# A bidirectional state-space mixer on one core: transposes on TensorE, stores off SP's queue, a moved sum, gates kept in DRAM, products on GpSimd

## The chip, the cores and the metric

The kernel runs on one core of a Trainium2 chip. The metric is the device time of one execution in microseconds (us). The kernel before was timed twice: 1167.71 and 1169.27 us, median 1168.49 us. Its trace comes from one further, profiled execution. The engines are named as in the profile: PE is TensorE, DVE is VectorE, ACT is ScalarE, POOL is GpSimd, SP is SyncE, which here only issues DMA (SPq is its queue of issues).

## What is computed

One pre-norm layer of a bidirectional state-space mixer over 1024 tokens of width 1024 (inner width 2048, 32 heads of 64 in 8 groups, state 128, chunks of 128 tokens), then a final norm:

```python
u = rmsnorm(x, norm_w)
proj = u @ w_in                       # 1024 x 6208
z, xbc, dt_raw = proj[..., :2048], proj[..., 2048:6144], proj[..., 6144:]
xbc = silu(depthwise_conv_centred(xbc, conv_w, conv_b))   # 5 taps
xs, bm, cm = x heads, B, C            # slices of xbc
dt = softplus(dt_raw + dt_bias); a = -exp(a_log)
y = xs * d_skip
for direction in range(2):            # 1: on flipped tokens
    y = y + ssd_scan(xs * dt, dt * a, bm, cm)     # chunked scan
y = y * silu(z)                       # the gate
y = y * rsqrt(mean(y*y per group) + EPS) * ssd_norm_w
out = rmsnorm(x + y @ w_out, final_norm_w)
```

## The kernel before

All products of float32 matrices are made of three matmuls on pairs of a rounded "hi" part and a "lo" rest: hi·hi, hi·lo, lo·hi. ACT casts the hi part (L129) and DVE or POOL subtracts it for the lo part (L130).

**Start** (0 to 75 us of the trace). x is normed and transposed into four blocks b11, b12, b21, b22 (channel half by token half); sums of blocks t1 to t4 are made, and the z gate of group 0 and dt are projected. b12 and this gate go to DRAM (`b12_d`, `gate_d`).

**Product phase** (75 to 514 us). The 4096 columns of x, B and C come in 16 pairs of 128-column tiles: for each group g first "BC" (one tile of B, one of C), then "x" (two tiles). `load_pair` loads a pair's weights on SP (L261) into `raw`, which has two buffers, one pair ahead, and makes seven combinations a11, s1, s2, a12, s3, s4, a22 (POOL's sums L273, ACT's casts, DVE's and POOL's lo parts). `pair_products` is a 2x2 block scheme with seven products of twelve 128x512 matmuls each (L295). They accumulate in two PSUM tiles c1 and c2 of 1024 columns, halves c11, c12, c21, c22. Product P5 (from s1 and t1) lies in a PSUM tile of its own and is copied to SBUF as `p5` (L324). Between products DVE adds `p5` to c12 (L330), ACT copies c12 to c22 (L331), and later DVE writes c21 = c22 − p5 (L335): the next product accumulates onto what these wrote. Then `conv` filters c1 and c2: one pass of ACT (L344), four of DVE (L350), tanh on ACT (L353), the closing product on DVE (L354). `keep_tm` turns x and B into token-major order: a DVE transpose in blocks of 32x32 (L362) and four DMAs on SP (L365) to `xb_d`, in pieces of 32 columns. B and C also go to `bc_d`, on SP (L463).

**Gap** (514 to 546.6 us). After the last pair b12 comes back from DRAM (L475), the gates of group 0 too (L640), and the z weights of group 1 (L484) are loaded and split.

**Scan phase** (546.6 to 1029 us). `z_stream` makes the z columns of groups 1 to 7: eight steps a group, each 24 matmuls 128x256 (L145). `gate_of` puts the gates into SBUF tiles of four chunks. `ssd_units(g)` yields 16 times: eight backward steps and eight forward chunks. A `state` multiplies xb by wdt to xw on DVE (L530) and PE multiplies it (L533); `update` carries the running state (L523, L525). `mix` makes the decay matrix of a chunk on ACT (L557, L562) and DVE (L559, L567). A forward chunk then makes pyo and pyd on PE (L600, L606), adds on DVE (L609, L619), multiplies by the gate on DVE (L624), takes the norm (square on ACT L626, power on POOL L85, scale on ACT L628), transposes on DVE (L631) and stores to `y_d` with four DMAs on SP (L634). z steps stand between the yields, at positions given by the tuple AT. Of the sixteen units of the output product (48 matmuls 128x512 each, L709: eight token tiles by two halves of the inner width), four of half 0 stand in the last group.

**Tail** (1029 to 1161 us). The other twelve units.

The framework orders each engine's instructions by a priority, which `high_priority` moves ahead.

## Time and profile before

| | us |
|---|---|
| median of two runs | 1168.49 |
| the profiled execution, its own time | 1162.74 |
| its span in the trace | 1161.0 |
| PE busy | 950.8 (82%) |
| DVE busy | 835.4 (72%) |
| ACT busy | 585.2 (50%) |
| POOL busy | 253.0 (22%) |

The profiled execution took 1.74 us more than its span, and 5.75 us less than the median. Busy times of PE are upper bounds of useful work: successive matmuls overlap in the trace, so the start of one to the start of the next says more than a duration.

### The profile page before, as it was taken

How to read it: one execution, taken by the hardware profiler on the slowest of the kernel's cores; microseconds unless marked ns; L12 is line 12 of the kernel's file. 1: busy time of each engine (PE TensorE's matmuls, PEld its weight loads, DVE VectorE, ACT ScalarE, POOL GpSimd, SP SyncE). 2: the span in 40 equal slices, each digit the busy share in tenths (PEclk: the TensorE clock that was granted, in tenths of full speed). 3: DMA queues.
4: the chain of work that ended last, by engine and by line, in shares of the span. 5: the costliest groups of instructions: out<-in, count | busy, mean ns of one | idle time of the engine just before them, and what ended most of it. 6: DMA issues, size and time to landing. Idle time of an engine off the chain costs nothing.

```text
span 1161.0 us, 15429 instructions
## 1 busy us (share of the span) xinstructions
PE 950.8 (82%) x4890; PEld 798.0 (69%) x4890; DVE 835.4 (72%) x1687; ACT 585.2 (50%) x1573; POOL 253.0 (22%) x228
## 2 busy tenths in 40 slices
PE   4894689588958966861999998989887779999997
PEld 4783467466736755651999987879775557888886
DVE  5547879848866884873789888888888886855423
ACT  4442344244334422421687877787877673744211
POOL 4359531245145304500000100010111000010000
PEclk9797899889979998995999999999995688999999
DMA  7221134433372345138766665676667657868531
GB/s 220 86 92 36 46 97 103 91 91 72 73 169 55 68 91 127 18 73 249 197 187 166 158 166 144 152 169 163 174 156 166 147 155 211 186 183 295 177 109 55
DMA packets 272915, 155.90 MB, mean 134 GB/s; under 512 B 176752, under 2 KB 244032, under 8 KB 272320
## 3 DMA queue, kind: packets, MB, share of 16 engines
q1 hardware_dynamic: 272832, 154.90, 51.0%
q8 instruction: 39, 0.64, 0.2%
q14 instruction: 44, 0.36, 0.1%
HBM read 113.70 MB, written 41.16 MB: 133 GB/s over the span
## 4 chain that ended last, share of the span: by engine, by line
PE 48%; DVE 18%; ACT 11%; DMA 8%; issue 7%; POOL 6%; SPq 1%; DVEq 0%; POOLq 0%; ACTq 0%
PE po L709 14%; PE x L295 9%; PE pz L145 9%; PE BC L295 6%; DMA fb<-rows_d 5%; PE pyd L606 3%; DVE x L350 3%; PE pyo L600 2%; ACT yo L617 2%; DVE B L350 2%; ACT fb L557 2%; PE sb L533 2%; DMA wz<-in_ssd_w_in_dram 2%; DVE C L350 2%; ACT fb L562 1%
## 5 line engine op out<-in xcount | busy, mean ns | idle before, releaser
L617 ACT ACTIVATE yo<-pyo,ecs 128x64 f32<-128x64 f32 x448 | 103.8, 310 | 19.5 <-PE pyo L600 16.9
L557 ACT ACTIVATE fb<-fb,cfb 128x128 f32<-128x128 f32 x256 | 83.2, 396 | 27.9 <-DMA fb<-rows_d 27.7
L562 ACT ACTIVATE fb<-fb,cfb 128x128 f32<-128x128 f32 x256 | 85.1, 394 | 21.6 <-DVE fb L559 21.3
L350 DVE SCALAR_TENSOR_TENSOR x<-x,prm,x 128x1022 f32<-128x1022 f32 (+1 forms) x64 | 81.7, 1276 | 14.9 <-ACT x L344 13.7
L606 PEld LDWEIGHTS pyd<-xb,mt 128*128 128x128 f32 x512 | 73.4, 214 | 19.8 <-ACT pyd L626 14.6
L609 DVE SCALAR_TENSOR_TENSOR y<-xb,coef,pyd 128x64 f32<-128x64 f32 x256 | 61.6, 272 | 32.5 <-PE pyd L606 32.3
L606 PE MATMUL pyd<-xb,mt 128*128 128x64 f32 x512 | 74.8, 295 | 11.5 <-ACT pyd L626 8.9
L559 DVE COPY_PREDICATED fb<-trif,fb 128x512 f32<-128x512 uint32 x64 | 47.1, 736 | 11.3 <-ACT fb L557 11.1
L145 PE MATMUL pz<-wz_0h,b11h 128*128 128x256 f32 (+1 forms) x60 | 20.1, 334 | 35.3 <-ACT wz_0h L129 32.4
L600 PE MATMUL pyo<-pf,ct 128*128 128x256 f32 x112 | 38.4, 426 | 12.7 <-DVE pf L525 9.8
L619 DVE TENSOR_TENSOR y<-y,yo 128x256 f32<-128x256 f32 x112 | 46.6, 417 | 3.1 <-ACT yo L617 2.9
L709 PE MATMUL po<-wo0h,yh 128*128 128x512 f32 x128 | 45.9, 434 | 2.5 <-ACT yh L129 2.5
L709 PE MATMUL po<-wo0l,yh 128*128 128x512 f32 x128 | 44.4, 427 | 2.6 <-DVE wo0l L664 2.6
L533 PE MATMUL sf<-xwf,xb 128*128 128x256 f32 x112 | 39.4, 437 | 8.2 <-ACT yo L617 6.0
L709 PE MATMUL po<-wo0h,yl 128*128 128x512 f32 x128 | 44.4, 422 | 1.9 <-DVE yl L130 1.9
L85 POOL TENSOR_TENSOR y_0r<-y_0m,neghalf 128x1 f32<-128x1 f32 x8 | 4.8, 603 | 188.3 <-DVE y_0m L82 188.3
L567 DVE TENSOR_TENSOR mt<-fb,pcb 128x512 f32<-128x512 f32 x64 | 43.4, 678 | 3.3 <-ACT fb L562 2.9
L350 DVE SCALAR_TENSOR_TENSOR B<-BC,prm,B 128x1022 f32<-128x1022 f32 (+1 forms) x32 | 40.9, 1279 | 2.8 <-ACT B L344 2.2
L533 PE MATMUL sb<-xwb,xb 128*128 128x256 f32 x112 | 38.0, 429 | 5.6 <-issue 2.2
L709 PE MATMUL po<-wo1h,yh 128*128 128x512 f32 (+1 forms) x136 | 42.2, 377 | 0.0
L709 PE MATMUL po<-wo1l,yh 128*128 128x512 f32 (+1 forms) x136 | 42.1, 377 | 0.0
L709 PE MATMUL po<-wo1h,yl 128*128 128x512 f32 (+1 forms) x136 | 42.1, 377 | 0.0
(1402 smaller groups left out, 3165.8 us busy)
## 6 DMA issues: line engine op xcount, KB each, us to landing
fb<-rows_d SPq DMA_DIRECT2D x128, 256.0 KB, 4.4
xb<-xb_d SPq DMA_DIRECT2D x64, 192.0 KB, 4.1
wz<-in_ssd_w_in_dram SPq DMA_DIRECT2D x16, 512.0 KB, 5.3
y_d<-yt SPq DMA_DIRECT2D x256, 32.0 KB, 2.3
wo<-in_ssd_w_out_dram SPq DMA_DIRECT2D x16, 512.0 KB, 4.9
...
```

Of the source, the lines that this page charges most:

```text
L145: nc.tensor.matmul(pz[:, 0:m], a, b, start=at == 0, stop=at == 3 * NK - 1)
L295: nc.tensor.matmul(ps, a[:, k, :], b[:, k, :], start=fresh and n == 0, stop=n == 11, skip_group_check=True)
L350: nc.vector.scalar_tensor_tensor(out=acc[:, o], in0=ps[:, i], scalar=w(k), in1=acc[:, o], op0=ALU.mult, op1=ALU.add)
L533: nc.tensor.matmul(ps[:, 0:CW], xb[:, CW:CW + P], xw, start=True, stop=True)
L557: nc.scalar.activation(out=ef[:, h], in_=ef[:, h], func=AF.Identity, bias=cfb[:, 1, c, hsl(g, h)])
L559: nc.vector.copy_predicated(ef, trif.bitcast(U32).unsqueeze(1).broadcast_to([P, HG, P]), fb[:, 0])
L562: nc.scalar.activation(out=ef[:, h], in_=ef[:, h], func=AF.Exp, bias=cfb[:, 0, c, hsl(g, h)])
L600: nc.tensor.matmul(pyo[:, d * CW:(d + 1) * CW], ct[:, tok], st, start=True, stop=True)
L606: nc.tensor.matmul(pyd[:, cs], mt[:, h, :], xb[:, cs], start=True, stop=True)
L609: nc.vector.scalar_tensor_tensor(out=y[:, cs], in0=xb[:, cs], scalar=coef[:, h:h + 1], in1=pyd[:, cs], op0=ALU.mult, op1=ALU.add)
L617: nc.scalar.activation(out=yo[:, cs], in_=pyo[:, d * CW + h * HD:d * CW + (h + 1) * HD], func=AF.Copy, scale=ecs[:, d, c, hsl(g, h)])
L709: nc.tensor.matmul(pos[i], l_, r_[:, cols[i]], start=k == 0 and a == 0, stop=k == NO - 1 and a == 2)
```

## The change

- **Turning.** `keep_tm` transposes x and B by eight matmuls against the identity on PE into two PSUM tiles, which ACT copies to SBUF (L371); one DMA on ACT's queue stores the tile in pieces of 128 columns. The stores of B and C to `bc_d` are issued by ACT too. This part is deferred: the transposes of a pair's two tiles stand in the next pair, after its fourth and its seventh product (`late`).
- **P5.** ACT copies c12 to c22 and c22 to c21 with nothing between; DVE adds `p5` to c12 and to c22 once, after the pair's products, ahead of the convolution (L341, L342).
- **Order of the combinations and tiles.** s2 and s4 are summed earlier; the sums share the ring of the weight tiles (10 for hi, 12 for lo).
- **End of the product phase.** The reload of b12 and the first z weights stand ahead of the last pair's convolution.
- **Gates.** All gates go to `gate_d` by DMAs issued by POOL (L526) and come back on SP, one chunk at a time (64 loads, L626).
- **Scan.** xw (112 operations) and y times gate (64) are on POOL. The transpose and store of a chunk's y stand behind the next chunk's scaling. xb has 8 buffers, not 9.
- **Fillers.** The z stream, the loads of the first half's w_out and the units of half 0 are one generator `fills`, which yields every 12 matmuls within a unit; AT has ten places a group, not eight. FIRST = 5 units of half 0 stand in the scan, not 4.

```diff
@@ load_pair
         put("a11", a11, False)
         s1 = combine("s1", a21, a22, ALU.add)
+        s2 = combine("s2", s1, a11, ALU.subtract)
         put("s1", s1, False)
-        s2 = combine("s2", s1, a11, ALU.subtract)
         put("s2", s2, False)
...
@@ pair_products
         product(c11, w["a12"], b21, False)
+        late(0)
         c2 = ptile(name + "2", w)
         c21, c22 = c2[:, 0:512], c2[:, 512:1024]
         with tc.high_priority(offset=HP):
-            nc.vector.tensor_tensor(out=c12, in0=c12, in1=p5, op=ALU.add)
             nc.scalar.copy(c22, c12)
         product(c22, w["s3"], t3, False)
         product(c12, w["s4"], b22, False)
         with tc.high_priority(offset=HP):
-            nc.vector.tensor_tensor(out=c21, in0=c22, in1=p5, op=ALU.subtract)
+            nc.scalar.copy(c21, c22)
         product(c21, w["a22"], t4, False)
-        return c1, c2
+        late(1)
+
+        nc.vector.tensor_tensor(out=c12, in0=c12, in1=p5, op=ALU.add)
+        return c1, c2, lambda: nc.vector.tensor_tensor(out=c22, in0=c22, in1=p5, op=ALU.add)
@@ keep_tm
-        tt = big(name, (P, 32, 32))
-        nc.vector.transpose(tt.rearrange("p b j -> p (b j)"), acc)
-        dst = xb_d[g].rearrange("(b i) c -> i b c", i=32)
-        for a in range(4):
-            nc.sync.dma_start(out=dst[:, :, off + 32 * a:off + 32 * a + 32],
-                              in_=tt[32 * a:32 * a + 32])
+        tm = big(name, (P, NC, P))
+        for q in range(2):
+            pt = pst(f"{name}p{q}")
+            for k in range(4):
+                nc.tensor.transpose(out=pt[:, k * P:(k + 1) * P],
+                                    in_=acc[:, (4 * q + k) * P:(4 * q + k + 1) * P], identity=ident)
+            nc.scalar.copy(tm[:, 4 * q:4 * q + 4], pt.rearrange("p (k n) -> p k n", k=4))
+        nc.scalar.dma_start(out=xb_d[g].rearrange("(k p) c -> p k c", p=P)[:, :, off:off + P], in_=tm)
@@ the loop over pairs
+                nc.scalar.dma_start(out=bc_d[g, i], in_=acc)
...
+        if nxt is None:
+
+            b12 = ublock(up, "v", "b12b")
+            for i, part in enumerate(b12):
+                nc.sync.dma_start(out=part.rearrange("p k t -> p (k t)").bitcast(F32), in_=b12_d[i])
+            wz1 = load_z(1)
...
+            if i:
+                join()
+            acc = conv(p_, 2 * g + i if nm == "x" else 16 + 8 * i + g, f"{nm}{i}_{g}")
+            left.append(keep(acc, g, nm, i))
@@ z_stream
+                        nc.gpsimd.dma_start(out=gate_d[g, :, c0:c0 + 4], in_=gt)
@@ state
-        nc.vector.tensor_tensor(out=h4(xw), in0=h4(xb[:, 0:CW]),
+        nc.gpsimd.tensor_tensor(out=h4(xw), in0=h4(xb[:, 0:CW]),
@@ ssd_units, a forward chunk
+            nc.sync.dma_start(out=gt, in_=gate_d[g, :, c])
...
-            nc.vector.tensor_tensor(out=y, in0=y, in1=gates[g, c // 4][:, c % 4], op=ALU.mult)
+            nc.gpsimd.tensor_tensor(out=y, in0=y, in1=gt, op=ALU.mult)
...
+            if c > 0:
+                store(c - 1, done)
+            done = y
@@ the order of the scan
-    AT = (2, 5, 8, 10, 11, 13, 14, 15)
-    every(stream, 2)
+    AT = (2, 6, 8, 9, 10, 11, 12, 13, 14, 15)
+    every(stream, 3)
```

How the change moves instructions. On SP in the middle of the product phase, the kernel before has the two halves of the load of wx2r (weights of pair x2) on both sides of group 1's last store and group 2's first ones:

```order
44 L365 DMA xb_d<-x1t_1469 32x32x32 x4
45 L261 DMA wx2r<-in_ssd_w_in_dram 128x8x128
46 L463 DMA bc_d<-B_1607 128x1024
47 L365 DMA xb_d<-Bt_1617 32x32x32 x4
48 L463 DMA bc_d<-C_1623 128x1024
49 L261 DMA wBC3r<-in_ssd_w_in_dram 128x8x128 x2
```

The same place of the changed kernel:

```order
28 L262 DMA wx2r<-in_ssd_w_in_dram 128x8x128 x2
29 L262 DMA wBC3r<-in_ssd_w_in_dram 128x8x128 x2
30 L262 DMA wx3r<-in_ssd_w_in_dram 128x8x128 x2
31 L262 DMA wBC4r<-in_ssd_w_in_dram 128x8x128 x2
32 L262 DMA wx4r<-in_ssd_w_in_dram 128x8x128 x2
```

No store stands between the weight loads of the pairs any more.

On SP at the end of the product phase, before:

```order
84 L365 DMA xb_d<-x0t_3336 32x32x32 x4
85 L365 DMA xb_d<-x1t_3351 32x32x32 x4
86 L475 DMA b12bh<-b_d 128x2048
87 L475 DMA b12bl<-b_d 128x2048
88 L640 DMA gate0r_3375<-gate_d 128x1024
89 L640 DMA gate0r_3377<-gate_d 128x1024
90 L484 DMA wz_0_3379<-in_ssd_w_in_dram 128x4x256
91 L484 DMA wz_1_3389<-in_ssd_w_in_dram 128x4x256
92 L540 DMA bt_3449<-bc_d 128x1024
```

and in the changed kernel:

```order
38 L262 DMA wx7r<-in_ssd_w_in_dram 128x8x128 x2
39 L442 DMA wz_0_3525<-in_ssd_w_in_dram 128x4x256
40 L442 DMA wz_1_3535<-in_ssd_w_in_dram 128x4x256
41 L442 DMA wz_0_3873<-in_ssd_w_in_dram 128x4x256
42 L442 DMA wz_1_3883<-in_ssd_w_in_dram 128x4x256
43 L494 DMA b12bh<-b_d 128x2048
44 L494 DMA b12bl<-b_d 128x2048
45 L442 DMA wz_0_4575<-in_ssd_w_in_dram 128x4x256
```

The z weights (wz) of group 1 stand right behind the last weight load, ahead of b12, and wait for no store.

On POOL in the first group's forward chunks the changed kernel has (the kernel before has only the rows of L85 there):

```order
176 L659 TENSOR_TENSOR y_0_3844<-y_0_3844,gt_0_3819 128x256
177 L85 TENSOR_TENSOR y_0r<-y_0m,neghalf 128x1
178 L553 TENSOR_TENSOR xwf_3_4151<-xb_3_3737,wdt 128x256
179 L659 TENSOR_TENSOR y_1_3943<-y_1_3943,gt_1_3917 128x256
180 L553 TENSOR_TENSOR xwf_4_4245<-xb_4_3701,wdt 128x256
181 L85 TENSOR_TENSOR y_1r<-y_1m,neghalf 128x1
182 L659 TENSOR_TENSOR y_2_4035<-y_2_4035,gt_2_4009 128x256
183 L553 TENSOR_TENSOR xwf_5_4337<-xb_5_3692,wdt 128x256
184 L526 DMA gate_d<-gate_4_3773 128x1024
```

xwf runs two chunks ahead of the gate's product there, and the store of a gate stands in the same queue.

## Rows read from the trace of the kernel before

**Rows 1.** Windows by stage: length; busy time (instructions) of PE, PEld, DVE, ACT, POOL; PEclk, DMA, GB/s.
```profile
159.00:514.00 355.00, 284.19 (x1152) 220.41 (x1152) 264.69 (x242) 133.89 (x186) 119.94 (x85) 0.93 0.38 86
514.00:546.00 32.00, 0.14 (x1) 0.00 (x0) 13.85 (x11) 3.41 (x4) 0.00 (x0) 0.57 0.57 160
546.00:1029.00 483.00, 432.20 (x2655) 382.70 (x2655) 401.68 (x1238) 354.44 (x1226) 42.08 (x62) 0.91 0.67 171
1029.00:1161.00 132.00, 125.43 (x572) 103.77 (x571) 53.43 (x75) 32.49 (x55) 7.13 (x10) 0.98 0.50 162
```

**Rows 2.** Timeline of PE: start, duration; first matmul of pair BC1, x7's last twelve.
```profile
159.24 0.50 PE L295 MATMUL BC<-b11h,wBC1a11h 128*128 128x512 f32 x1 [0.98 <-DVE C L350]
...
511.18 0.39 PE L295 MATMUL x<-t4h,wx7a22h 128*128 128x512 f32 x1
...
513.74 0.40 PE L295 MATMUL x<-t4h,wx7a22l 128*128 128x512 f32 x1
```

**Rows 3.** Waits of PE, 159 to 514 us: waiter, releaser: total, times, longest.
```profile
PE BC L295 <- ACT BC L331: 19.8, 7, 4.9
PE x L295 <- ACT wx6a11h L129: 14.2, 1, 14.2
...
PE x2w L295 <- ACT wx2s1h L129: 12.6, 1, 12.6
PE x L295 <- ACT x L331: 6.3, 5, 1.5
```

**Rows 4.** Timeline of SP, 215 to 245 us: start, duration of the issue.
```profile
217.97 2.23 SPq L365 DMA_DIRECT2D xb_d<-x1t  x4
220.25 0.62 SPq L261 DMA_DIRECT2D wx2r<-in_ssd_w_in_dram  x1
```

**Rows 5.** Timeline of POOL and of DVE, 224 to 240 us.
```profile
224.65 1.26 POOL L273 TENSOR_TENSOR wx2s<-wx2r 128x512 f32<-128x512 f32 x1 [31.09 <-DMA wx2r<-in_ssd_w_in_dram]
...
235.81 0.68 DVE L130 TENSOR_TENSOR wx2s1l<-wx2s,wx2s1h 128x512 fp32r<-128x512 f32 x1
...
237.02 1.77 DVE L130 TENSOR_TENSOR wx2a12l<-wx2r,wx2a12h 128x512 fp32r<-128x512 f32 x1
...
238.20 1.74 POOL L130 TENSOR_TENSOR wx2s4l<-wx2s,wx2s4h 128x512 fp32r<-128x512 f32 x1
```

**Rows 6.** Groups of DVE, 159 to 514 us: count | busy, mean ns | idle before.
```profile
L362 DVE STREAM_TRANSPOSE x1t<-x 128x1024 f32<-128x1024 f32 x7 | 8.7, 1246 | 0.2
```

**Rows 7.** Timeline of PE, 20 to 40 us: four 128x128 transposes a row.
```profile
30.38 1.11 PE L204 MATMUL pu<-ident,xt 128*128 128x128 f32 x4 [0.55 <-DVE t2l L130]
...
37.52 0.60 PE L204 MATMUL pu<-ident,xt 128*128 128x128 f32 x4
```

**Rows 8.** Timeline of all engines after the last product, 515 to 547 us.
```profile
519.03 1.23 DVE L354 SCALAR_TENSOR_TENSOR x<-x_7t,x 128x1024 f32<-128x1024 f32 x1 [1.17 <-ACT x_7t L353]
...
521.86 5.24 DVE L350 SCALAR_TENSOR_TENSOR x<-x,prm,x 128x1022 f32<-128x1022 f32 x4 [0.33 <-ACT x L344]
...
530.82 2.24 SPq L365 DMA_DIRECT2D xb_d<-x1t  x4
...
535.60 1.21 SPq L484 DMA_DIRECT2D wz<-in_ssd_w_in_dram  x2
...
546.58 0.58 PE L145 MATMUL pz<-wz_0h,b11h 128*128 128x256 f32 x1 [32.44 <-ACT wz_0h L129]
```

**Rows 9.** Groups of DVE, 546 to 1029 us: count | busy, mean ns | idle before.
```profile
L619 DVE TENSOR_TENSOR y<-y,yo 128x256 f32<-128x256 f32 x111 | 46.2, 416 | 3.1 <-ACT yo L617 2.9
...
L530 DVE TENSOR_TENSOR xwf<-xb,wdt 128x256 f32<-128x256 f32 x56 | 23.2, 418 | 1.1 <-PE sf L533 1.1
L624 DVE TENSOR_TENSOR y<-y,gate 128x256 f32<-128x256 f32 x55 | 22.9, 416 | 0.1
```

**Rows 10.** Timeline of POOL near the start: a 320-column operation.
```profile
12.59 0.87 POOL L130 TENSOR_TENSOR wz_3l<-wz,wz_3h 128x320 fp32r<-128x320 f32 x1 [0.23 <-ACT wz_3h L129]
```

**Rows 11.** One window inside the scan phase, columns as in rows 1.
```profile
866.00:922.00 56.00, 37.59 (x125) 27.12 (x125) 45.91 (x142) 38.86 (x139) 6.78 (x8) 0.63 0.67 157
```

More of the change, by code (lines that the diff above doesn't have):

```diff
@@ L312, in ptile, with pair_products @@
         return t_
-    def pair_products(w, name):
+    def pair_products(w, name, late):
         c1 = ptile(name + "1", w)
@@ L493, in z_stream, with psh @@
+    late(0)
+    late(1)
+    first.close()
+    bp = main.enter_context(tc.tile_pool(name="bp", bufs=2))
+    ps_h = ctx.enter_context(tc.tile_pool(name="ps_h", bufs=2, space=PSUM))
+    sp = main.enter_context(tc.tile_pool(name="sp", bufs=2, side="right"))
+    def psh(name):
+        return ps_h.tile([P, 512], F32, tag="h", name=name)
+    def z_stream(nxt):
         for g in range(1, NG):
@@ L577, in mix, with store @@
             mts[c] = mt, coef
+        def store(c, y):
+            yt = sp.tile([P, CW // 32, 32], F32, tag="yt", name=f"yt{g}_{c}", bufs=1)
+            nc.vector.transpose(yt.rearrange("p b i -> p (b i)"), y)
+            yg = y_d[g * CW:(g + 1) * CW, c * P:(c + 1) * P]
+            yg = yg.rearrange("(b j) (a i) -> a j b i", j=32, i=32)
+            for a in range(4):
+                nc.sync.dma_start(out=yg[a], in_=yt[32 * a:32 * a + 32])
         token_major(NC - 1)
@@ L591, in ssd_units @@
             xb = xbs.pop(c)
+            gt = sp.tile([P, CW], F32, tag="gate", name=f"gt{g}_{c}")
+            nc.sync.dma_start(out=gt, in_=gate_d[g, :, c])
             if c < NC - 1:
@@ L628, in ssd_units @@
             nc.scalar.activation(out=y, in_=y, func=AF.Copy, scale=r)
-            yt = sp.tile([P, CW // 32, 32], F32, tag="yt", name=f"yt{g}_{c}", bufs=1)
-            nc.vector.transpose(yt.rearrange("p b i -> p (b i)"), y)
-            yg = y_d[g * CW:(g + 1) * CW, tok].rearrange("(b j) (a i) -> a j b i", j=32, i=32)
-            for a in range(4):
-                nc.sync.dma_start(out=yg[a], in_=yt[32 * a:32 * a + 32])
-            yield
-    for i in range(2):
-        gates[0, i] = big(f"gate0r{i}", (P, 4, CW))
-        nc.sync.dma_start(out=gates[0, i], in_=gate_d[:, 4 * i:4 * i + 4])
-    stream = z_stream()
-    AT = (2, 5, 8, 10, 11, 13, 14, 15)
-    every(stream, 2)
-    for g in range(NG - 1):
-        work = ssd_units(g)
-        for i in range(2 * NC):
-            next(work)
-            every(stream, AT.count(i))
-        next(work, None)
-    every(stream, 2)
+            if c > 0:
+                store(c - 1, done)
+            done = y
+            if c == NC - 1:
+                store(c, done)
+            yield
     NO = DI // P // 2
@@ L710, in out_unit @@
                              start=k == 0 and a == 0, stop=k == NO - 1 and a == 2)
+            if half == 0 and j % 12 == 11 and j < 47:
+                yield
         if half == 0:
@@ L736, in out_unit, with finish, fills @@
         return nprep
[L738 to L753 removed]
+    def finish(work):
+        while True:
+            try:
+                next(work)
+            except StopIteration as end:
+                return end.value
+    FIRST = 5
+    wo1, preps = [], []
+    def fills():
+        yield from z_stream(wz1)
+        for k in range(NO):
+            if k % 2 == 0:
+                tiles = wo_tiles(up, 0, k // 2)
+            wo1.append(load_wo(tiles, 0, k))
+        prep = out_prep(0, 0)
+        for t in range(NC):
+            prep = yield from out_unit(0, t, wo1, prep, (0, t + 1) if t < NC - 1 else (1, 0))
+            preps.append(prep)
+            yield
+    stream = fills()
+    AT = (2, 6, 8, 9, 10, 11, 12, 13, 14, 15)
+    every(stream, 3)
+    for g in range(NG):
+        work = ssd_units(g)
+        for i in range(2 * NC):
+            next(work)
+            if len(preps) < FIRST:
+                every(stream, AT.count(i))
+        next(work, None)
+    while len(preps) < FIRST:
+        next(stream)
     main.close()
@@ L758 @@
     wo2 = []
-    for t in range(NC // 2, NC):
-        prep = out_unit(0, t, wo1, prep, (0, t + 1) if t < NC - 1 else (1, 0))
-        for _ in range(2):
+    for t in range(FIRST, NC):
+        while len(preps) < t + 1:
+            next(stream)
+        for _ in range(3):
+            if len(wo2) == NO:
+                break
             if len(wo2) % 2 == 0:
```

138 lines of the change are left out of this document (58 added, 80 removed).

## The prediction

> **What bounds the kernel now.** I read the busy time by stage first [rows 1]. PE is nearly always busy in the tail (125.4 of 132 us) and never in the gap (0.14 of 32). In the product phase it has 284.2 of 355 us, in the scan phase 432.2 of 483. So time can be won in three places, and for each I looked for what ends PE's waits.
>
> In the product phase from pair BC1 to the end of x7, 159.24 to 514.1 us, there are 14 pairs [rows 2], 25.35 us each. Twelve matmuls of a product start 0.233 us apart (511.18 to 513.74 is eleven steps), so 84 matmuls need 19.6 us. The waits of PE name two causes [rows 3]. Three single stalls on cast weights (12.6 us before x2, 14.2 before x4 and again, the same, before x6) come from SP: it issued the first half of wx2r at about 217, behind four stores of x1t, and the second at 220.25 [rows 4]; POOL, which needs it, sat idle for 31.09 us [rows 5]. The load stood in the queue behind stores that wait for DVE's transposes. The other cause is the chain DVE sum, ACT copy, next product: 19.8 + 6.3 us [rows 3]. Together 12.6 + 14.2 + 14.2 + 19.8 + 6.3 = 67.1 us.
>
> In the gap the last product ends at 514.1. Convolution and transposes of x7 follow, the last four stores are issued at 530.82, the z weights behind them at 535.60, and PE starts at 546.58 after 32.44 us [rows 8]. In the scan phase PE, DVE (401.7) and ACT (354.4) are all loaded [rows 1]; where fillers ran out, PE had 37.6 of 56 us at a granted clock of 0.63 while DVE had 45.9 [rows 11].
>
> **The change part by part, product phase.** No store stands among SP's weight loads after the change, so the three stalls, 41.0 us, should go: the cover is one pair (22 us) between load and use, and a load waits only for the casts of the pair two before. P5's sum leaves the chain: the copy c12 to c22 can run during the fourth product, c22 to c21 during the sixth, 2.8 us each (12 x 0.233) against ACT's copy; the 26.1 us of waits should go as well. DVE does the same two sums, later, so its work is unchanged there, but 24 transposes of 1.246 us [rows 6] go from DVE, 21 of them in this stretch: (264.7 − 26.1)/14 = 17.0 us a pair, below PE's need.
>
> PE gains twelve transposes a pair on average (eight for BC, sixteen for x). Four took 0.60 us at the better place and 1.11 at the worse [rows 7], so 1.8 to 3.3 us a pair; I take 1.8, since PE is busier here than at the start. ACT gains four copies of 512 columns a pair (three for transposed halves, one for c21), and 40 DMA issues in all. No DMA of ACT or POOL is in this trace; SP's issues cost 0.56 us each (2.23 for four) and 0.62 [rows 4]. At 0.3 to 0.62 us that is 12 to 25 us over the phase, on an engine with 133.9 of 355 us busy [rows 1]: hidden, unless it delays a copy by more than the 2.8 us of cover. Stretch: 354.9 − 67.1 + 14 x 1.8 = 313 us, or 22.3 a pair; the floor is 19.6 + 1.8 = 21.4, so 300.
>
> The deferred transposes are a new wait in PE's order: those of a pair's first tile stand 11.2 us into the next pair (four products of 2.8). The convolution must be through by then, and behind a stalled transpose stand all later products. DVE needs a sum of 512 columns (taken as a lo part's 0.68 [rows 5]), four passes (5.24), a wait for tanh and the closing product (1.17 and 1.23 [rows 8]) and two or three lo parts: 0.68 us each alone, 1.77 beside POOL [rows 5]. That is 10 to 11.5 us: it just fits. Ahead of BC1 two pairs lose three transposes (3.7 us of DVE): I take 155 instead of 159.2, with 0 to 8 as bounds. Last product then: 155 + 313 = 468.
>
> **Gap.** z weights and b12 no longer wait for x7's stores. What stays is that z needs a PSUM buffer which the convolution of x7 reads: a sum of 0.7 and four passes, 5.24, with a lo part or two between, some 8 us after the last product (32.5 before). Below, 3 if the first sum is early; above, 20 if the first xb and xw come late, since the first sb stands ahead of z on PE.
>
> **Scan phase.** xw and the gate's product leave DVE: 23.2 (xwf), as much for xwb, and 26.6 for 64 gates at 0.416 [rows 9], 73 us. POOL took 0.87 us for 320 columns [rows 10] and 1.26 for 512 [rows 5]; the line through both gives 0.74 for 256, an estimate, so 176 x 0.74 = 130 us, beside 42.1 of its own [rows 1]: 172 of some 460, room enough. Queued behind the gate's product is POOL's power for the norm, which ACT's scale waits for; y's transpose and store stand one chunk later on DVE and SP, so this hop has cover. xwf runs two chunks ahead. The gate's stores wait on POOL for DVE's `gate_of`; 64 more loads cost SP 0.3 to 0.62 us each, 20 to 40 us of the phase; SP does nothing else than issue, so I count nothing for it.
>
> The cost of this move is contention. A DVE lo part with two SBUF operands took 1.77 beside POOL, 0.68 alone, and POOL's took 1.74 instead of 1.26 [rows 5]. DVE keeps 272 operations with two SBUF operands (64 of L559, one a chunk, 112 of L619 [rows 9], 96 of L523). If POOL is busy 37% of the time and each meeting costs half a POOL operation: 272 x 0.37 x 0.37 = 37 us. The least is 0, the most is that every moved operation holds DVE for its whole length, 130. Net for DVE: −73 + 37 = −36.
>
> One more output unit stands here: the tail has twelve in 132 us, so 11.0. The phase was 482.5 (546.6 to 1029); PE's busy time plus a unit, 432.2 + 11 = 443, is a floor, and 482.5 + 11 = 494 is what comes if the lighter DVE buys nothing. I take 482.5 − 36 + 11 = 458, since DVE kept its mean load (45.9 of 56, 0.82) in the slice where PE waited [rows 11], and AT's ten places put z and units there. (PE's busy time counts overlaps of matmuls, so its floor is soft.)
>
> **Tail.** 132 − 11 = 121.
>
> **Sum.** 468 + 8 + 458 + 121 = 1055 of span, 1057 with the 1.74 around it. The median before stands 5.75 above that execution: 1062.
>
> **A rule against the change.** The measured meeting in rows 5 lengthens DVE by 1.09 us and POOL by 0.48. The Trainium skill, SBUF — State Buffer, "Summary: rules for kernel authors", says that when VectorE has two SBUF inputs while a GpSimd operation reads SBUF, the second to issue fully blocks until the first finishes. Rows 5 agree with it. By that rule my 37 us is the random-meeting case, and rival 4 below is the case in which all meet.
>
> **Rivals.** 1) *The pace of pairs stays*: the deferred transposes or ACT's longer queue hold PE as the sums did. For it: the 10 to 11.5 us against 11.2, and ACT in order. Against: the three long stalls have a cause that is gone. 155 + 14 x 25.35 = 510, 42 us more: 1104.
> 2) *The scan gets no shorter*: the hop over POOL and meetings eat the 36 us. For it: 176 added hops between engines. 494 for 458: 1098.
> 3) *Both phases reach PE's floor*: 300 and 443: 13 + 15 less, 1034.
> 4) *The other side: POOL locks DVE out.* Every moved operation blocks DVE for its whole length: DVE 402 − 73 + 130 = 459 at its present share of 0.83 is 553 us, 1157 in all, within 2% of before. If they also lengthen as in rows 5 (1.74 for 1.26) they take 180: 509/0.83 = 613, total 1217, slower. It decides at a phase of 587 us (1192 in all), where a moved operation costs DVE 0.91 us. Against: much of DVE's work in a chunk reads PSUM (L609, L567, L525), and the meeting in rows 5 is one of operands that all lie in SBUF.
>
> **How the numbers follow.** My case 0.56 (1040 to 1085), rival 1 0.15, rival 2 0.13, rival 3 0.10, rival 4 0.06, half of it slower. The likeliest gives 1062. The range 1022 to 1110 takes in rivals 1 to 3 apart, leaving out rival 4, rivals 1 and 2 together (1140) and the lowest edge of rival 3. About 2% is what a measurement can tell: faster 0.93 (all but rival 4 and a little), same 0.04, slower 0.03.
>
> **What would show it.** In the trace after: SP's loads of weights with no POOL wait of 31 us; no wait of PE on the copies longer than 1 us; pairs 22.3 us apart; first z matmul 8 us behind the last product; DVE in the scan near 366 us with L619 above 0.416; POOL near 172. Wrong would be: PE waiting for the deferred transposes' tile (rival 1), DVE still over 400 in the scan or its partners at a multiple of 0.416 (rivals 2, 4), PE waiting for xw or for loads behind the gates on SP.

## The result and the profile after

The changed kernel takes 1127.99 us (two runs, 1127.91 and 1128.08) for 1168.49 before: 0.965 of it, 95% interval 0.961 to 0.970. That is faster, as forecast, but 66 us slower than the 1062 predicted and 18 above the range. The profiled execution's span is 1126.1 us.

The page's first row and the busy time by stage (length; PE, PEld, DVE, ACT, POOL; PEclk, DMA, GB/s), which answer to [rows 1]:

```profile
PE 977.5 (87%) x5082; PEld 816.6 (73%) x5082; DVE 783.6 (70%) x1487; ACT 619.1 (55%) x1637; POOL 377.3 (34%) x424
...
150.00:448.00 298.00, 295.41 (x1347) 237.72 (x1345) 245.43 (x231) 168.86 (x256) 116.08 (x89) 1.00 0.39 119
448.00:458.00 10.00, 0.75 (x3) 0.66 (x3) 8.67 (x8) 3.31 (x4) 1.79 (x2) 0.72 0.98 337
458.00:1020.00 562.00, 487.01 (x2832) 418.02 (x2830) 388.38 (x1077) 360.55 (x1233) 174.06 (x252) 0.90 0.70 181
1020.00:1126.00 106.00, 91.12 (x408) 74.02 (x408) 42.16 (x55) 26.36 (x41) 4.38 (x8) 0.95 0.43 140
```

The fourteen pairs from BC1 on take 298 us instead of 355, with PE busy for 295.4 of them at a granted clock of 1.00 of full speed (0.93 before); the gap takes 10 instead of 32.5. From the first z matmul (457.9) on, the kernel is slower than before: 668.2 us to the end of the span for 614.4 (1161.0 − 546.6). 88.7 us were won up to there and 53.8 given back.

PE's timeline (start, duration) at both ends of the product phase, which answers to [rows 2] and [rows 8]:

```profile
150.32 0.48 PE L295 MATMUL BC<-b11h,wBC1a11h 128*128 128x512 f32 x1
...
447.54 0.40 PE L295 MATMUL x<-t4h,wx7a22l 128*128 128x512 f32 x1
457.25 1.22 PE L556 MATMUL sb<-xwb,xb 128*128 128x256 f32 x2 [9.31 <-POOL xwb L553]
457.91 0.78 PE L146 MATMUL pz<-wz_0h,b11h 128*128 128x256 f32 x1
```

297.6 us for fourteen pairs are 21.26 each. PE's waits of 150 to 448 us (total, times, longest), for the 67.1 us of [rows 3]; this is the longest of seven, all of this kind:

```profile
PE x0t_0p L369 <- DVE x L359: 0.8, 1, 0.8
PE x0t_1p L369 <- DVE x L359: 0.3, 1, 0.3
```

Nothing is left there but the deferred transposes waiting 0.3 us, once 0.8, for the convolution. In the gap the trace shows what ends PE's wait: SP issues the eight xb loads at 449.78 and POOL then makes xwb.

```profile
449.78 5.84 SPq L568 DMA_DIRECT2D xb<-xb_d  x8
...
455.98 1.79 POOL L553 TENSOR_TENSOR xwb<-xb,wdt 128x256 f32<-128x256 f32 x2 [37.73 <-DMA xb<-xb_d]
```

### The profile page after: what moved, and what is told of

The parts are those of the page before. It is cut to its first block, busy times and chain, and to the rows that moved or that the text cites. A ratio compares the mean times of both kernels' runs of the same rounds, so it can differ in the third digit from the quotient of the medians.

```text
span 1126.1 us, 16040 instructions
## 1 busy us (share of the span) xinstructions
PE 977.5 (87%) x5082; PEld 816.6 (73%) x5082; DVE 783.6 (70%) x1487; ACT 619.1 (55%) x1637; POOL 377.3 (34%) x424
## 4 chain that ended last, share of the span: by engine, by line
PE 52%; DVE 11%; issue 11%; DMA 9%; ACT 9%; POOL 7%; SPq 1%; POOLq 0%; DVEq 0%; ACTq 0%
PE x L295 12%; PE po L728 11%; PE BC L295 8%; DMA fb<-rows_d 6%; PE pz L146 5%; PE pyd L641 4%; POOL y L659 2%; PE pyo L635 2%; ACT fb L585 2%; ACT fb L580 2%; PE sf L556 1%; ACT yo L652 1%; DMA wo<-in_ssd_w_out_dram 1%; DMA wz<-in_ssd_w_in_dram 1%; PE pcb L588 1%
## 5 line engine op out<-in xcount | busy, mean ns | idle before, releaser
L659 POOL TENSOR_TENSOR y<-y,gt 128x256 f32<-128x256 f32 x64 | 55.3, 864 | 162.5 <-ACT fb L585 59.2
L580 ACT ACTIVATE fb<-fb,cfb 128x128 f32<-128x128 f32 x256 | 83.1, 394 | 48.2 <-DMA fb<-rows_d 43.6
L641 PE MATMUL pyd<-xb,mt 128*128 128x64 f32 x512 | 78.8, 305 | 26.9 <-ACT pyd L661 15.6
L585 ACT ACTIVATE fb<-fb,cfb 128x128 f32<-128x128 f32 x256 | 82.8, 395 | 20.4 <-DVE fb L582 19.9
L355 DVE SCALAR_TENSOR_TENSOR BC<-BC,prm,BC 128x1022 f32<-128x1022 f32 (+1 forms) x64 | 82.0, 1281 | 6.9 <-ACT BC L349 5.6
L644 DVE SCALAR_TENSOR_TENSOR y<-xb,coef,pyd 128x64 f32<-128x64 f32 x256 | 55.4, 276 | 44.2 <-PE pyd L641 44.0
L553 POOL TENSOR_TENSOR xwb<-xb,wdt 128x256 f32<-128x256 f32 x56 | 37.8, 684 | 95.0 <-DMA xb<-xb_d 48.7
L553 POOL TENSOR_TENSOR xwf<-xb,wdt 128x256 f32<-128x256 f32 x56 | 37.6, 674 | 88.7 <-PE sf L556 61.3
L582 DVE COPY_PREDICATED fb<-trif,fb 128x512 f32<-128x512 uint32 x64 | 49.8, 779 | 19.6 <-ACT fb L580 19.1
L590 DVE TENSOR_TENSOR mt<-fb,pcb 128x512 f32<-128x512 f32 x64 | 43.6, 683 | 21.9 <-ACT fb L585 21.1
L661 ACT ACTIVATE pyd<-y 128x256 f32<-128x256 f32 x64 | 24.7, 385 | 37.4 <-POOL y L659 36.9
L588 PE MATMUL pcb<-ct,bt 128*128 128x128 f32 x128 | 30.3, 326 | 16.8 <-ACT pyd L661 13.8
```

The lines of the kernel that those rows point to most:

```text
L355: nc.vector.scalar_tensor_tensor(out=acc[:, o], in0=ps[:, i], scalar=w(k), in1=acc[:, o], op0=ALU.mult, op1=ALU.add)
L553: nc.gpsimd.tensor_tensor(out=h4(xw), in0=h4(xb[:, 0:CW]), in1=bc4(wdt[:, d, c, g * HG:(g + 1) * HG], HD), op=ALU.mult)
L580: nc.scalar.activation(out=ef[:, h], in_=ef[:, h], func=AF.Identity, bias=cfb[:, 1, c, hsl(g, h)])
L585: nc.scalar.activation(out=ef[:, h], in_=ef[:, h], func=AF.Exp, bias=cfb[:, 0, c, hsl(g, h)])
L641: nc.tensor.matmul(pyd[:, cs], mt[:, h, :], xb[:, cs], start=True, stop=True)
L644: nc.vector.scalar_tensor_tensor(out=y[:, cs], in0=xb[:, cs], scalar=coef[:, h:h + 1], in1=pyd[:, cs], op0=ALU.mult, op1=ALU.add)
```

## The experiments

All times are medians of four executions (two for the changed kernel), with the kernel before beside them; its median in the five groups of runs was 1163.7 to 1167.0 us, so differences of runs from different groups are taken between ratios, times 1165 us.

For the scan I read one more number from every trace, the *transitions*: from the start of a group's last y transpose on DVE to the next group's first pyd matmul, summed over seven. Where the next group's backward steps run under the forward chunks, it is small or negative. *Forward* is the rest: from a group's first pyd to its last y transpose, summed over eight groups. The two trade: a backward step that runs under a chunk leaves the transitions and lengthens forward. So their sum says more of a run than either column.

| kernel | median us | ratio (95%) | forward | transitions | after the last chunk |
|---|---|---|---|---|---|
| before | 1168.5 | 1 | 455 | 15 | 123 |
| changed | 1128.0 | 0.965 (0.961 to 0.970) | 500 | 38 | 106 |
| e4, the base | 1081.3 | 0.928 (0.923 to 0.932) | 460 | 12 | 126 |
| e5, base + DRAM gates | 1114.6 | 0.957 (0.953 to 0.961) | 466 | 46 | 124 |
| e10, base + loads only | 1115.7 | 0.957 (0.954 to 0.961) | 461 | 48 | 124 |
| e9, base + stores (POOL) | 1097.6 | 0.940 (0.936 to 0.945) | 485 | 4 | 129 |
| e18, base + stores (SP) | 1104.6 | 0.948 (0.947 to 0.950) | 454 | 37 | 130 |
| e13, e5 with loads on POOL | 1100.9 | 0.947 (0.942 to 0.951) | 478 | 4 | 130 |
| e6, base + late store | 1071.7 | 0.921 (0.919 to 0.923) | 468 | −2 | 123 |
| e8, base + xw and gate on POOL | 1095.8 | 0.941 (0.940 to 0.943) | 503 | −14 | 123 |
| e16, e6 + xw on POOL | 1063.9 | 0.913 (0.909 to 0.918) | 488 | −31 | 124 |

### What in the scan costs the time: four runs

**e1.** xw and the gate's product back on VectorE.

```diff
-        nc.gpsimd.tensor_tensor(out=h4(xw), in0=h4(xb[:, 0:CW]),
+        nc.vector.tensor_tensor(out=h4(xw), in0=h4(xb[:, 0:CW]),
-            nc.gpsimd.tensor_tensor(out=y, in0=y, in1=gt, op=ALU.mult)
+            nc.vector.tensor_tensor(out=y, in0=y, in1=gt, op=ALU.mult)
```

> The changed kernel with xw and y times gate back on VectorE, all else as changed. Changed kernel: 1128.0 us, its scan and output phases together (first z matmul to the end) 668 us against 614.5 before. Theory A (the hop over GpSimd lengthens the chain of every chunk): the time falls by 40 to 55 us, to 1073 to 1088. Theory B (the new order of fillers scatters the units of the output product and leaves nothing to cover the second half's weights): no more than 10 us either way, 1118 to 1138. Theory C (gates through DRAM and the delayed store hold SyncE's queue): also 1118 to 1138.

1118.2 us (0.959, 0.954 to 0.963): 8 less than the changed kernel. Theory A falls as the main cause.

**e2.** The order of fillers of before, the rest as changed.

```diff
-    AT = (2, 6, 8, 9, 10, 11, 12, 13, 14, 15)
-    every(stream, 3)
+    AT = (2, 5, 8, 10, 11, 13, 14, 15)
+    every(stream, 2)
...
+        if i in (5, 9, 11, 13):
+            prep = finish(out_unit(0, t, wo1, prep, (0, t + 1)))
```

> The changed kernel with the order of fillers of the kernel before: two z steps ahead, eight a group, four units of the output product in the last group at its positions 5, 9, 11, 13, twelve in the tail with two weight loads each; xw, gate and store as changed. Theory A: 1118 to 1138. Theory B: falls by 40 to 55 us, to 1073 to 1088. Theory C: 1118 to 1138.

1139.8 us (0.977, 0.973 to 0.982): slower than the changed kernel. The new order is a gain of some 14 us here, so theory B falls as the main cause.

**e3.** The kernel before with xw and gate on GpSimd.

```diff
-            nc.vector.tensor_tensor(out=y, in0=y, in1=gates[g, c // 4][:, c % 4], op=ALU.mult)
+            nc.gpsimd.tensor_tensor(out=y, in0=y, in1=gates[g, c // 4][:, c % 4], op=ALU.mult)
```

(and xw likewise)

> The kernel before (1168.5 us) with xw and y times gate on GpSimd and nothing else changed. Theory A: longer by 40 to 55 us, 1208 to 1224. Theories B and C: within 12 us of 1168, and rather shorter, since VectorE loses 73 us of work.

1185.3 us (1.017, 1.013 to 1.021). A real price of 19 us, less than half of what theory A wanted.

**e4, the base.** The product phase and gap of the change, the scan of before.

```diff
-                        nc.gpsimd.dma_start(out=gate_d[g, :, c0:c0 + 4], in_=gt)
-            nc.sync.dma_start(out=gt, in_=gate_d[g, :, c])
+            gt = gates[g, c // 4][:, c % 4]
-            if c > 0:
-                store(c - 1, done)
+            store(c, y)
```

(with the edits of e1 and e2)

> The changed kernel's product phase and gap (transposes on TensorE, stores on ScalarE's queue, the moved sum, z weights early) with everything of the scan as before: xw and gate on VectorE, gates in SBUF, old order of fillers, store not delayed; only xb keeps 8 buffers. All theories: the product phase ends near 448 and z starts near 458 as in the changed kernel; if the scan then takes its old 614.5 us, the time is 458 + 614.5 + 7.5 = 1080. If the loss of the scan came from the earlier start itself (clock, transfers), it stays near 1128.

1081.3 us, 1080 foretold. So the loss does not come from the earlier start: the product phase and the gap are worth 84 us and the changes of the scan cost 44. That the forecast was met so closely is partly luck. The first z matmul came at 455.0, not 458; the way to the end took 624.0 us, not 614.5; and the median lies 2.3 us above the profiled span, where 7.5 had been added. Whether the 10 us come from the earlier start or from xb's eight buffers for nine, no run separates. Its scan and end, lines as above:

```profile
455.00:953.50 498.50, 443.80 (x2700) 390.95 (x2701) 408.82 (x1247) 355.15 (x1227) 45.30 (x64) 0.91 0.66 166
953.50:1079.00 125.50, 118.45 (x542) 98.11 (x540) 49.10 (x63) 30.77 (x49) 4.38 (x8) 0.98 0.49 163
```

### The parts of the scan, one by one on the base

**e5.** Gates stored to and loaded from DRAM, as in the changed kernel.

```diff
+                        nc.gpsimd.dma_start(out=gate_d[g, :, c0:c0 + 4], in_=gt)
...
-            gt = gates[g, c // 4][:, c % 4]
+            gt = sp.tile([P, CW], F32, tag="gate", name=f"gt{g}_{c}")
+            nc.sync.dma_start(out=gt, in_=gate_d[g, :, c])
```

> The product phase of the change with the scan of before (1081 us) plus one part: all gates stored to DRAM on GpSimd's queue and loaded back chunk by chunk on SyncE. Theory C1 (the 64 loads stand in SyncE's order ahead of the loads of the decay rows and hold them until an old gate buffer is free): 20 to 40 us more, 1100 to 1120, with more waits of ScalarE for the decay rows. If C1 is wrong: 1076 to 1086.

1114.6: 35 us more. This is the largest single part. But C1's sign came only in small measure: ACT's waits for the decay rows (fb), 455 to 960 us, first in the base, then in e5:

```profile
ACT fb L584 <- DMA fb<-rows_d: 39.4, 23, 9.0
```

```profile
ACT fb L580 <- DMA fb<-rows_d: 47.8, 26, 8.8
```

That is 8 us. Below, C1 stands for SP's order in general.

**e6.** The delayed store.

```diff
-            store(c, y)
+            if c > 0:
+                store(c - 1, done)
+            done = y
+            if c == NC - 1:
+                store(c, done)
```

> The same base (1081 us) plus one part: transpose and store of a chunk's y stand one chunk later. Theory C2 (the delay holds y's two buffers longer and puts the stores into SyncE's order where later loads wait for them): 15 to 40 us more. If C2 is wrong: 1071 to 1086, a little less because VectorE no longer waits for the scaled y.

1071.7: 8 us less. C2 falls; the delay is a gain.

**e7.** The changed kernel with both products on VectorE and no delay (new fillers, DRAM gates).

```diff
-            if c > 0:
-                store(c - 1, done)
-            done = y
-            if c == NC - 1:
-                store(c, done)
+            store(c, y)
```

(and the edits of e1)

> The changed kernel with xw and gate on VectorE and the store not delayed: the new order of fillers and gates in DRAM stay. The run with both on VectorE and the store delayed took 1118 us. If the delay costs nothing: 1113 to 1123. If C2 holds: 1080 to 1103. Against the run with DRAM gates and old fillers it gives the price of the new order of fillers: theory B more than 10 us, else less.

1112.7 us (0.958, 0.955 to 0.961), the same as e5: without the GpSimd part the new order of fillers is worth nothing measurable, and with DRAM gates the delay gains nothing (e1, which has it, has the same ratio, 0.959).

**e8.** xw and gate on GpSimd, as in e3, on the base.

```diff
-            nc.vector.tensor_tensor(out=y, in0=y, in1=gt, op=ALU.mult)
+            nc.gpsimd.tensor_tensor(out=y, in0=y, in1=gt, op=ALU.mult)
```

(and xw likewise)

> The same base (1081 us) plus one part: xw and y times gate on GpSimd. Theory A as measured on the kernel before (1185 for 1167): 1095 to 1103. If the shorter product phase changes what bounds the scan: within 5 us of 1081.

1095.8: 16 us more, as on the kernel before.

### Why the loads cost so much

**e9.** The 14 stores alone; the gate is still read from SBUF.

```diff
                         gate_of(gt, pz)
+                        nc.gpsimd.dma_start(out=gate_d[g, :, c0:c0 + 4], in_=gt)
```

> The base (product phase of the change, scan of before, 1081 us) with the 14 stores of the gates to DRAM on GpSimd's queue added; the multiplication still reads the gates in SBUF, so these stores are extra work that nobody reads. Theory C1 (the loads on SyncE are what costs 33 us): 1077 to 1087. Theory C3 (the stores are: on GpSimd they wait for a gate of VectorE, and the powers of the norm queue behind them): 1100 to 1118.

**e10.** The 64 loads alone.

```diff
-            gt = gates[g, c // 4][:, c % 4]
+            gt = sp.tile([P, CW], F32, tag="gate", name=f"gt{g}_{c}")
+            nc.sync.dma_start(out=gt, in_=gate_d[0, :, c])
```

> The base with the 64 loads of gates on SyncE, and no stores: every group is multiplied by the gates of group 0 from DRAM, so groups 1 to 7 get another gate than the reference's; z products and gates are made as ever and then not read. Theory C1: 1100 to 1118. Theory C3: 1077 to 1087. If it is each in part: between.

Stores alone 1097.6 (+14, between the ranges of C1 and C3), loads alone 1115.7 (+34, as much as both, so the parts do not add). The table says where: with the loads on SP the forward part is unchanged (461 for 460) and the transitions grow by 36 us, which is all of the loss. PE in e10 at the change from group 3 to group 4 (DVE transposed group 3's last y at 702.11):

```profile
699.18 0.60 PE L555 MATMUL sb<-xwb,xb 128*128 128x256 f32 x2
700.11 0.70 PE L555 MATMUL sb<-xwb,xb 128*128 128x256 f32 x2 [0.34 <-DVE pb L547]
702.25 0.79 PE L555 MATMUL sb<-xwb,xb 128*128 128x256 f32 x2 [1.43 <-DVE pb L547]
703.58 1.22 PE L555 MATMUL sb<-xwb,xb 128*128 128x256 f32 x2 [0.54 <-DVE pb L547]
706.56 1.22 PE L634 MATMUL pyo<-pb,ct 128*128 128x256 f32 x2 [1.76 <-DVE pb L547]
...
711.23 1.81 PE L640 MATMUL pyd<-xb,mt 128*128 128x64 f32 x8
```

The backward steps (sb, most waiting for DVE's update pb) stand alone, and the first pyd comes 9.1 us after that transpose. In the base its counterpart came before it (705.58 and 706.40):

```profile
705.58 1.81 PE L644 MATMUL pyd<-xb,mt 128*128 128x64 f32 x8
...
706.40 0.44 DVE L610 STREAM_TRANSPOSE yt<-y 128x256 f32<-128x256 f32 x1
```

SP's order accounts for it. In the base, group 4's first load of xb stands ahead of the store of group 3's *first* chunk; with the gate loads in the queue it stands behind the store of its *fifth* (rows of the programs' orders; `yt_n` is the transposed y of chunk n, `xb_7_6838` and `xb_7_6898` are group 4's):

```
base:  154 L572 DMA xb_7_6838<-xb_d 128x384        loads: 190 L609 DMA y_d<-yt_4_6642 32x8x32 x4
       155 L614 DMA y_d<-yt_0_6230 32x8x32 x4             191 L625 DMA gt_7_6836<-gate_d 128x256
                                                          193 L567 DMA xb_7_6898<-xb_d 128x384
```

13 of the 36 us lie in the last transition (21.1 for 8.0), where loads of w_out stand in the same queue.

**e13** takes the loads to GpSimd's queue, after which SP's order is the base's again.

```diff
-            nc.sync.dma_start(out=gt, in_=gate_d[g, :, c])
+            nc.gpsimd.dma_start(out=gt, in_=gate_d[g, :, c])
```

> The base with gates through DRAM (1114.6 us) with its 64 loads issued by GpSimd instead of SyncE; the instruction order of SyncE is then that of the base, where each group's first xb load stands ahead of the store of the group before's first chunk. Theory C1 (SyncE's order): falls by 14 us or more, to 1081 to 1100, the backward steps hidden again. Theory C4 (the transfers and their latency): stays, 1107 to 1122. Against C1 counts only a result over 1105.

1100.9 us: 13 less than e5, where C1 wanted 14 or more, and the transitions fall from 46 to 4. Forward grew by 12, in part because the backward steps are under the chunks again; the sum of both falls from 512 to 482, with 472 in the base. That is C1's mechanism. Stores and loads on POOL keep a price of 22 us over the base, where the stores alone cost 14 (e9).

**e14** makes 16 loads of 64, with the same bytes.

```diff
-            gt = sp.tile([P, CW], F32, tag="gate", name=f"gt{g}_{c}")
-            nc.sync.dma_start(out=gt, in_=gate_d[g, :, c])
+            if c % 4 == 0:
+                g4 = big(f"gt{g}_{c}", (P, 4, CW))
+                nc.sync.dma_start(out=g4, in_=gate_d[g, :, c:c + 4])
+            gt = g4[:, c % 4]
```

> The base with gates through DRAM (1114.6 us) with 16 loads of four chunks on SyncE instead of 64 of one; the same bytes. SyncE's order has the next group's loads later than the base, but less than with 64. Theory C1: 1085 to 1105. Theory C4 with cost by bytes: stays, 1107 to 1122; with cost by transfer count: 1085 to 1095.

1110.4 us (0.954, 0.950 to 0.958): no clear gain. This is outside C1's range (1085 to 1105) and inside C4's for a cost by bytes (1107 to 1122), so it speaks against C1 as the whole cause. Transitions fall to 22, but forward grows to 482, and their sum only falls from 512 to 504; why, no run shows. **e15**, the changed kernel with these loads and both products on VectorE (the fillers, against e14):

```diff
-    AT = (2, 5, 8, 10, 11, 13, 14, 15)
+    AT = (2, 6, 8, 9, 10, 11, 12, 13, 14, 15)
```

(and the delayed store)

> The changed kernel (new order of fillers, delayed store) with xw and gate's product on VectorE and gates loaded by fours. If the prices add: 1118 (both on VectorE) less what loading by fours saves, 1090 to 1105. If the new order of fillers needs the room that the gate loads took: below 1075.

1101.0 us (0.945, 0.939 to 0.950): 16 us better than e1, and still 37 behind the fastest kernel.

**e18.** The unread stores of e9 issued by SP.

```diff
-                        nc.gpsimd.dma_start(out=gate_d[g, :, c0:c0 + 4], in_=gt)
+                        nc.sync.dma_start(out=gate_d[g, :, c0:c0 + 4], in_=gt)
```

> The base with the 14 unread stores of gates (1097.6 us from GpSimd) issued by SyncE. If it was GpSimd's queue (the power of the norm behind a store that waits for a gate): 1079 to 1088. If it is the store itself, wherever it is issued (the gate's tile, the order, the transfers): 1092 to 1103.

1104.6, more than from GpSimd (1097.6) and just above both ranges. On SP the loss stands in the transitions (37 for 12, forward 454), on POOL in the chunks (485 for 460), and the sums are nearly the same (491 and 489, base 472). It is not the powers of the norm in POOL's queue alone.

### What of the GpSimd part costs

**e16**: xw alone, on e6.

```diff
-        nc.vector.tensor_tensor(out=h4(xw), in0=h4(xb[:, 0:CW]),
+        nc.gpsimd.tensor_tensor(out=h4(xw), in0=h4(xb[:, 0:CW]),
```

> The fastest kernel so far (base with the delayed store, 1071.7 us) with xw alone on GpSimd. If the 14.5 us of the GpSimd part come from the gate's product (in the chain from pyd to the square that frees its PSUM buffer): 1062 to 1074. If they come from xw (in the chain of the backward steps): 1080 to 1088.

**e17**: the gate's product alone, on the base.

```diff
-            nc.vector.tensor_tensor(out=y, in0=y, in1=gt, op=ALU.mult)
+            nc.gpsimd.tensor_tensor(out=y, in0=y, in1=gt, op=ALU.mult)
```

> The base (1081 us) with y times gate alone on GpSimd, xw on VectorE. If the gate's product carries the loss and xw is worth 8 us there too: 1098 to 1108. If the loss comes from both together (GpSimd's queue with two kinds of work): 1081 to 1090.

e16: 1063.9 us, the fastest kernel of the study, 9 us less than e6. e17: 1083.1 (0.930, 0.928 to 0.931), 2 more than the base. Alone, xw on GpSimd gains (on e6, with the delayed store) and the gate's product costs next to nothing (on the base); together, on the base, they cost 16. No run has xw alone without the delay, or both with it, so the delay's share in this is open. The waits of the scan (455 to 945 us) show the gate's hop and PE's waits for the buffer behind it, in e8:

```profile
ACT pyd L664 <- POOL y L662: 36.7, 41, 3.4
...
PE pcb L592 <- ACT pyd L664: 25.8, 25, 3.0
...
PE pyd L644 <- ACT pyd L664: 8.5, 11, 1.7
```

and in e17:

```profile
ACT pyd L664 <- POOL y L662: 27.0, 38, 3.7
...
PE pcb L592 <- ACT pyd L664: 12.1, 16, 1.9
...
PE pyd L644 <- ACT pyd L664: 7.7, 11, 1.7
```

In the base DVE's product stood there, with 8.8 us in six waits. ACT's square (L664) reads the gated y and frees pyd's PSUM buffer, so POOL's hop is in the chain from chunk to chunk. With xw in the same queue the hop is longer (36.7 for 27.0), and PE waits 34.3 us for such a buffer instead of 19.8 (13.4 in the base). That this difference makes the 16 us is argued from these waits, not shown by a run.

### The product phase

**e11.** P5's sum back in the chain of products, on the base.

```diff
+            nc.vector.tensor_tensor(out=c12, in0=c12, in1=p5, op=ALU.add)
             nc.scalar.copy(c22, c12)
...
-            nc.scalar.copy(c21, c22)
+            nc.vector.tensor_tensor(out=c21, in0=c22, in1=p5, op=ALU.subtract)
...
-        nc.vector.tensor_tensor(out=c12, in0=c12, in1=p5, op=ALU.add)
-        return c1, c2, lambda: nc.vector.tensor_tensor(out=c22, in0=c22, in1=p5, op=ALU.add)
+        return c1, c2, lambda: None
```

> The base with one part of the product phase undone: VectorE adds P5 to c12 before ScalarE's copy and makes c21 by a subtraction, as before. My prediction put these waits at 26 us in 14 pairs, 1.9 a pair; so last product at 474 instead of 448 and the time 1100 to 1110. If VectorE has room enough now that its transposes are gone and no wait builds up: 1081 to 1088.

1097.1 us: 16 more, between the two ranges; the last product ends at 464.5 instead of 448.5. PE's waits, 150 to 450 us:

```profile
PE BC L295 <- ACT BC L334: 9.9, 7, 2.4
PE x L295 <- ACT x L334: 3.1, 6, 0.5
```

The mechanism is right, with 13.0 us of waits and not 26.1. DVE has no transposes between any more, which may be why; no run shows it.

**e12.** The product phase's stores on SP again.

```diff
-        nc.scalar.dma_start(out=xb_d[g].rearrange("(k p) c -> p k c", p=P)[:, :, off:off + P], in_=tm)
+        nc.sync.dma_start(out=xb_d[g].rearrange("(k p) c -> p k c", p=P)[:, :, off:off + P], in_=tm)
```

(and the stores of B and C)

> The base with another part undone: the stores of x, B and C of the product phase are issued by SyncE again, between the weight loads (still one 128-column-piece DMA a tile, still deferred). My prediction: weight loads wait behind stores and the three stalls of 41 us come back: 1110 to 1125. If what made the stores late was VectorE's transposes, which are gone: 1080 to 1090.

1082.1 us: 1 more, and no stall. SP's waits, 150 to 450 us:

```profile
SPq L477 <- DVE BC L359: 57.5, 7, 8.8
SPq L372 <- ACT Bt L371: 39.6, 8, 9.0
```

SP still waits, but never more than 9.0 us, against a load issued a whole pair ahead. In the kernel before, one of its waits for a store took 31.7 us (SP's waits, 159 to 514 us):

```profile
SPq L365 <- DVE x0t L362: 72.7, 6, 31.7
```

So the stores may stand on SP here, as long as none waits that long. What shortened the wait (no transposes on DVE, one DMA a tile instead of four, the deferred stores) e12 does not separate.

## Why the prediction was wrong, step by step

**What bounds the kernel: right for two of three places.** In the product phase and in the gap time was won. In the scan phase, where PE waits as well, this change lost it.

**The sum.** In span the forecast was 1055 and 1126.1 was measured, 71 more: 20 less in the product phase, 2 more in the gap, 89 more in the scan phase and tail. That the median misses by 66 and not by 89 is luck: the product phase made up for 20, and the 5.75 us that I added from the profiled execution to the median did not come (0.08).

**Product phase: right in kind, too small.** The forecast was 155 + 14 x 22.3 = 468; it came to 150.3 + 14 x 21.26 = 447.9, at PE's floor (rival 3). The waits of 67.1 us went down to 2.6 (0.8 and six of 0.3), as said. The start at BC1 came 9 us earlier, not 4, just outside the bounds of 0 to 8. The transposes cost PE some 1.5 us a pair with these waits, for 1.8; eight of them delay the next product by 0.79 us where PE is busy (timeline of PE):

```profile
144.76 1.03 PE L369 MATMUL Bt_0p<-ident,BC 128*128 128x128 f32 x8
145.55 0.48 PE L295 MATMUL x<-b22l,wx0s4h 128*128 128x512 f32 x1
```

The rest lies in a term that I left standing. 354.9 − 67.1 is 288, and 14 pairs of 19.6 need 274. 11 of these 14 us stood behind six waits of 3.8 us and more, after each of which the trace before has seven to eleven matmuls more than 0.25 us apart, as here (0.43 for 0.233):

```profile
237.57 0.63 PE L295 MATMUL x2w<-t1l,wx2s1h 128*128 128x512 f32 x1
238.00 0.63 PE L295 MATMUL x2w<-t1h,wx2s1l 128*128 128x512 f32 x1
```

They went with the waits, and the mean granted clock of the stretch rose from 0.93 to 1.00. P5's chain is worth 16 us once the rest is changed (e11), not 26. The step that stands corrected is the cause of the three stalls: SP's queue was only where a store's long wait became a load's; with that wait gone, e12 has no stall on the same queue.

**Gap: 8 forecast, 10.0 measured**, and by the cause that was named for the upper bound: PE's order has sb of the first group ahead of z, and xb and xw come last.

**Scan phase and tail: wrong, by 89 us.** Forecast 458 + 121 = 579 from the first z matmul, measured 668. Of the 89, 36 are the gain that did not come, 44 are what the scan's changes cost against the base, and 10 are what the base's own scan and tail are longer than before (624.0 for 614.4). Three steps failed.

The first is the sentence on the 64 loads, "SP does nothing else than issue, so I count nothing for it". On the base they cost about 35 us (e5, e10); no run takes them alone out of the changed kernel. I priced their issue and asked who waits on SP for a transfer; I did not ask what stands behind them in SP's order. The next group's loads do, and with them the backward steps that PE used to do under the chunks. My signs of being wrong name "loads behind the gates on SP", but no term of the sum and no rival has a price for them.

The second is the step from DVE's load to the time, −73 + 37 = −36 taken off the phase. On the base the move alone (e8) took 27 us off DVE's busy time in the scan (408.8, in the base's line), and the kernel became 16 us slower. e8's scan:

```profile
455.00:971.00 516.00, 452.69 (x2710) 390.94 (x2711) 381.35 (x1072) 357.42 (x1229) 171.34 (x240) 0.90 0.64 162
```

In the changed kernel DVE's load fell from 401.7 to 388.4, not to 366, with more units to serve in the scan. DVE's load was not what set the pace. That −36 comes near the 27 is luck, since both of its terms were too large. Operations overlap on DVE: in the trace before, their durations add up to 493 us in 401.7 us busy, and without the moved ones it would be busy for 352, 50 less and not 73. And contention was far below 37 us. The three kinds that I had counted, in the changed kernel's scan:

```profile
L582 DVE COPY_PREDICATED fb<-trif,fb 128x512 f32<-128x512 uint32 x64 | 49.8, 779 | 19.6 <-ACT fb L580 19.1 <-DMA xb<-xb_d 0.2
L654 DVE TENSOR_TENSOR y<-y,yo 128x256 f32<-128x256 f32 x112 | 48.9, 437 | 2.4
...
L546 DVE TENSOR_TENSOR pb<-pb,dcy 128x256 f32<-128x256 f32 x48 | 25.6, 533 | 8.8 <-ACT pb L544 7.7
L546 DVE TENSOR_TENSOR pf<-pf,dcy 128x256 f32<-128x256 f32 x48 | 21.6, 449 | 5.8 <-ACT pf L544 5.6
```

Against the base (736, 419, 417 and 417 ns) that is 2.8 + 2.0 + 5.6 + 1.5 = 12 us. It is not that few met: by their times in the trace 95 of the 272 met a moved product, 35% for the 37% assumed. But GpSimd's operation was the first only 60 times, and DVE's then took 0.19 us longer on average, not 0.37. One such meeting:

```profile
711.24 0.72 POOL L659 TENSOR_TENSOR y<-y,gt 128x256 f32<-128x256 f32 x1
711.37 0.88 DVE L546 TENSOR_TENSOR pb<-pb,dcy 128x256 f32<-128x256 f32 x1
```

The Trainium skill's rule that the second of such a pair fully blocks until the first finishes (SBUF — State Buffer, "Summary: rules for kernel authors") fits this row: pb took 0.88 us for 0.42 and ended 0.29 us after the gate's product. Rival 4, built on it as if all met, falls. The moved operations themselves came out near the estimate of 0.74:

```profile
L659 POOL TENSOR_TENSOR y<-y,gt 128x256 f32<-128x256 f32 x64 | 55.3, 864 | 162.5 <-ACT fb L585 59.2 <-DVE y L654 53.6 <-issue 20.8
L553 POOL TENSOR_TENSOR xwf<-xb,wdt 128x256 f32<-128x256 f32 x56 | 37.6, 674 | 88.7 <-PE sf L556 61.3 <-DVE y L654 7.7 <-PE sb L556 4.6
```

That is 2.1 and 1.6 times DVE's 0.42. What the waits show as costly is the hop of the gate's product in the chain that frees pyd's buffer. I had looked at the hop behind it, from POOL's power to ACT's scale, and taken the delayed store as its cover; ACT's square, which waits for the product itself, has no such cover. Rival 2 names the hop, but lets it no more than eat the 36 us; e8 measured a net loss of 16 and e3 of 19.

The third is the place of the units. I counted five in the scan. The framework's order had more of the first half's units ahead, and 384 of their 384 matmuls ran before 1020 us, so the tail had eight units and the scan three more than I counted, about 33 us of work. The tail did not fall by as much. Its 408 matmuls would need 94 us at the pace of the tail before (132 us for 572), and it took 106. PE stood at its start for the second half's weights, of which theory B had spoken:

```profile
1025.40 1.62 PE L728 MATMUL po<-wo1h,yh 128*128 128x512 f32 x3 [6.19 <-ACT wo1h L682]
```

Not all is settled. On the base the parts are +35 (DRAM gates), +16 (GpSimd), −8 (delay), by their ratios 1123 us together; e2, which has these three and the old fillers, has a ratio that gives 1138, and the new fillers brought it to 1125. The 15 us between sum and e2 are an interplay of parts that no run separates (GpSimd's queue then holds xw, gate products, powers and stores). Nor is it shown why 14 stores that nobody reads cost 14 us on GpSimd and 24 on SP.
